# Two fused transformer blocks on one core: the keys' products regrouped by pairs of k-tiles under the modulation

## The chip, the cores and the metric

The kernel runs on one core of a Trainium2 chip, alone. The metric is device time in microseconds (us), the median of several executions; lower is better. Beside it stands one profiled execution, from which all rows below come.

## The reference

Two blocks follow each other. The first takes tokens `x` and a context `ctx`, each 256 x 1024, and two conditioning vectors, `c` and `c_ctx`. Cut to what the change touches:

```python
shift, scale, gate = split(silu(c) @ w_mod + b_mod)        # the same for c_ctx
h   = rmsnorm(x,   norm_w) * (1 + scale)   + shift
hc  = rmsnorm(ctx, norm_w) * (1 + scale_c) + shift_c
qkv, beta, decay, kb, vb = split(h @ w_state)              # the same for hc
q, k, v = silu(short_conv(qkv))                            # 4 heads of 128, conv of 5 taps
k = l2norm(k)
g, bt = gates(decay, beta)                                 # softplus, cumulative sums
o = gated_delta_rule(q, k, v, g, bt)                       # chunks of 64, both directions
...
x = x + gate * merge(...)
```

The second block (two feed-forward layers and a mixer, twice) takes `x` from there. It is not touched.

## The kernel before, in words

Everything is held transposed: 1024 features are 8 k-tiles (`KD`) of 128 partitions, and the 256 tokens (`T`) lie along the free axis. A product in fp32 accuracy is made of three fp32r matmuls: the weight is split into a high and a low part (`wload`: `wh` by an ACT copy, L98, `wl` by a DVE subtraction, L99) and so is the hidden tile (`split`, L289 and L290); `mm3` (L110 to L112) adds low x high, high x high and high x low. Weights arrive as panels of 512 KB (`wraw`, L90) through a ring of 7 buffers `raw`, issued by SP, and `wh` and `wl` have 4 buffers each. PSUM is 8 banks: `pj` 2, `ms` 2, `ch` 3, `md` 1.

The code is written in one order, and a scheduler then fixes one order of instructions for each engine. An engine works through its own list strictly in that order, so an instruction that waits holds up all that stand behind it on the same engine. `high_priority` (around the gates, the keys' convolution and the inverse) moves instructions ahead in those lists.

The first block opens with `b1_hidden`. `mod_row` (L729, L730) spreads silu(c) over all partitions. `mods(g)` makes shift and scale of two k-tiles, for g = 0 to 3: half of the shifts by multiply-and-reduce on DVE (L930), the rest by fp32 matmuls with the two conditioning columns `cc` as the stationary operand and a weight panel streaming (L943, result on 2 partitions), copied by ACT (L945) and transposed back (L948). `stats` squares the input (L155), sums the squares over features (`pss`, L165), takes the power on POOL (L170), spreads the result (`rb`, L173) and scales (L921). `hidden(g, ...)` applies scale and shift on ACT (L960) and splits.

Then come `b1_bd`, 48 products of 16 columns for the gates' inputs (L1022); `gates`, a chain of small DVE operations that ends in `gg` (L1111 to L1127), with sums over time on PE (`gps`, L1133; `gdf`, L1150) and exponentials `E` on ACT (L1151); and `b1_keys`, which for each of 4 heads takes 48 matmuls from `b1_both` (x and ctx, 8 k-tiles, 3 products), a convolution (`conv`: one ACT copy, L981, four DVE taps, L985, on both inputs at once), the halves of the key in chunk order (`conv_out`, L1001, or a silu on ACT for head 3, L999), 4 transposes (`ktp`, L1067), 4 squares with a sum (`ksq`, L1068) and 2 copies (L1069). `nke` (L1072) needs the sums of all four heads. From it follow `gc`, the products `Mc` (L1254), the triangular inverse of 32 x 32 blocks by 62 DVE operations `stmp` and `XW` (L1272, L1273), and the assembly of the full inverse on PE (`gx`, L1319; `gy`, L1325). Beside this chain PE works through two more such double products `w_kv` (each takes a `pj` bank), the four of `w_v`, and the 32 of `w_rest`.

```python
ps = self.b1_both(A["w_k"][h], hx, hc)      # b1_keys, per head
...
with self.tc.high_priority(offset=150):     # its convolution, transposes and squares
```

## Time and profile before

| what | value |
|---|---|
| median of 3 runs | 1453.55 us (1453.52 to 1453.86) |
| the profiled execution, its own time | 1454.4 us |
| span of its trace | 1452.6 us |
| PE busy | 1414.5 us, 97% of the span |
| DVE busy | 1149.1 us, 79% |
| ACT busy | 757.1 us, 52% |
| mean granted clock of PE | 0.995 |

The profile gives a page (busy time, 40 slices, the chain that ended last, the costliest groups) and answers to queries: the timeline of a stretch, the windows (busy time of each engine in given stretches), the waits of an engine by what ended them. Matmuls are pipelined: the duration of one is longer than its distance to the next, and PE counts as busy in both. The pace of PE is therefore read from starts, not from durations. An fp32 matmul leaves two records (two passes), an fp32r matmul one.

### The profile page before, as it was taken

To read this page: it belongs to the slowest core of one execution; us is meant where nothing else is said; L and a number is where in the kernel's file an instruction comes from. 1 tells how busy PE (TensorE), PEld (TensorE's weight loads), DVE (VectorE), ACT (ScalarE), POOL (GpSimd) and SP (SyncE) were. 2 spreads that over 40 slices of the span, in tenths; PEclk is the share of its full clock that TensorE was granted. 3 is DMA by queue.
4 is the path that set the end of the run, shared out by engine and by line. 5 is a ranking of instruction groups with operands and counts; after the bars stand their busy time and mean duration, and the time that the engine had idled before them with its cause. 6 is when DMAs were issued, how large, how long until landed. Compare 5 with 4: busy or idle time off the path is not lost. (4 is left out here: it accounts for less than half of the span.)

```text
span 1452.6 us, 27299 instructions
## 1 busy us (share of the span) xinstructions
PE 1414.5 (97%) x10738; PEld 1314.7 (91%) x10738; DVE 1149.1 (79%) x2130; ACT 757.1 (52%) x1285; POOL 90.4 (6%) x94
## 2 busy tenths in 40 slices
PE   7999889999999999999999999999999999999998
PEld 4799877789999988998899998999989998899997
DVE  6769777788887887898898788877778889896554
ACT  4653574354654455646664445554446347654442
POOL 0010100001300001001010001000001000100000
PEclk9999999999999999999999999999999999999999
DMA  8524544365688897456659898688775557577562
GB/s 325 183 60 124 152 131 120 99 197 187 213 261 278 298 320 226 160 160 215 205 151 318 279 337 263 185 282 290 244 242 180 174 168 240 173 241 245 177 197 70
DMA packets 94832, 303.96 MB, mean 209 GB/s; under 512 B 18128, under 2 KB 20432, under 8 KB 94448
## 3 DMA queue, kind: packets, MB, share of 16 engines
q1 hardware_dynamic: 89824, 299.90, 63.2%
q8 instruction: 84, 1.38, 0.4%
q10 hardware_dynamic: 4432, 1.11, 0.4%
q0 software_dynamic: 448, 1.21, 0.3%
q14 instruction: 44, 0.36, 0.1%
HBM read 300.09 MB, written 2.10 MB: 208 GB/s over the span
## 5 line engine op out<-in xcount | busy, mean ns | idle before, releaser
L98 ACT CAST wh<-raw 128x1024 fp32r<-128x1024 f32 (+3 forms) x407 | 414.6, 1021 | 280.7 <-PE psd L121 90.8
L99 DVE TENSOR_TENSOR wl<-raw,wh 128x1024 fp32r<-128x1024 f32 (+3 forms) x407 | 481.5, 1187 | 93.4 <-ACT wh L98 92.3
L111 PE MATMUL psf<-hH,wh 128*128 128x256 f32 x1088 | 306.1, 281 | 0.0
L112 PE MATMUL psf<-hL,wh 128*128 128x256 f32 x1088 | 305.6, 281 | 0.0
L110 PE MATMUL psf<-hH,wl 128*128 128x256 f32 x1088 | 305.5, 281 | 0.0
L121 PE MATMUL psd<-gHL,wh 128*128 128x512 f32 x704 | 244.3, 392 | 0.0
L739 DVE CUSTOM_DVE_ANT_0 raw<-raw,mrow 128x1024 f32<-128x1024 f32 x152 | 184.3, 1219 | 60.1 <-DMA raw<-in_wmod 59.8
L110 PEld LDWEIGHTS psf<-hH,wl 128*128 128x128 f32 x1088 | 205.6, 189 | 0.0
L112 PEld LDWEIGHTS psf<-hL,wh 128*128 128x128 f32 x1088 | 205.5, 189 | 0.0
L111 PEld LDWEIGHTS psf<-hH,wh 128*128 128x128 f32 x1088 | 204.8, 188 | 0.0
L122 PE MATMUL psd<-gHL,wl 128*128 128x256 f32 x704 | 196.8, 280 | 0.0
L121 PEld LDWEIGHTS psd<-gHL,wh 128*128 128x128 f32 x704 | 132.2, 188 | 29.1
L110 PE MATMUL psp<-hH,wl 128*128 128x256 f32 x512 | 148.9, 291 | 2.8 <-DVE wl L99 2.3
L111 PE MATMUL psp<-hH,wh 128*128 128x256 f32 x512 | 147.8, 289 | 0.0
L112 PE MATMUL psp<-hL,wh 128*128 128x256 f32 x512 | 147.4, 288 | 0.0
L122 PEld LDWEIGHTS psd<-gHL,wl 128*128 128x128 f32 x704 | 132.1, 188 | 0.0
L110 PEld LDWEIGHTS psp<-hH,wl 128*128 128x128 f32 x512 | 97.4, 190 | 5.0 <-PE psp L112 1.6
L112 PEld LDWEIGHTS psp<-hL,wh 128*128 128x128 f32 x512 | 97.3, 190 | 1.1 <-issue 0.7
L111 PEld LDWEIGHTS psp<-hH,wh 128*128 128x128 f32 x512 | 97.0, 189 | 0.4 <-issue 0.2
L249 ACT ACTIVATE ft<-psf 128x256 f32<-128x256 f32 x68 | 26.1, 383 | 110.0 <-PE psf L112 110.0
L157 POOL TENSOR_TENSOR sqa<-sqa,sq 128x256 f32<-128x256 f32 x36 | 31.2, 866 | 591.9 <-issue 480.6
L110 PE MATMUL psk<-hH,wl 128*128 128x256 f32 x160 | 46.7, 292 | 2.3 <-DVE cvv L985 2.3
(517 smaller groups left out, 2805.0 us busy)
## 6 DMA issues: line engine op xcount, KB each, us to landing
raw<-in_ffn_gu SPq DMA_DIRECT2D x176, 512.0 KB, 4.4
raw<-in_wmod SPq DMA_DIRECT2D x144, 512.0 KB, 4.5
raw<-in_ffn_dn SPq DMA_DIRECT2D x64, 448.0 KB, 4.2
raw<-in_win SPq DMA_DIRECT2D x56, 512.0 KB, 4.4
raw<-in_w_rest SPq DMA_DIRECT2D x32, 512.0 KB, 3.7
raw<-in_ffn_dn SPq DMA_DIRECT2D x32, 512.0 KB, 4.5
raw<-in_wmod_sc SPq DMA_DIRECT2D x12, 512.0 KB, 8.3
raw<-in_wout_a SPq DMA_DIRECT2D x16, 384.0 KB, 3.8
```

What stands on the lines that cost most here:

```text
L98: nc.scalar.copy(H[:, :n], raw[:, :n])
L99: nc.vector.tensor_sub(L[:, :n], raw[:, :n], H[:, :n].bitcast(F32))
L110: mm(ps, L[:, s], hH[:, b, :T], start=f, stop=False)
L111: mm(ps, H[:, s], hH[:, b, :T], start=False, stop=False)
L112: mm(ps, H[:, s], hL[:, b, :T], start=False, stop=l)
L121: mm(ps, H[:, s], h[:, b, :, :T], start=first and i == 0, stop=False)
L122: mm(ps[:, 1, :], L[:, s], h[:, b, 0, :T], start=False, stop=last and i == len(kw) - 1)
L157: self.seng.tensor_add(self.sqa, self.sqa, o)
L249: nc.scalar.activation(t, ps[:, 0, :], AF.Silu)
L739: nc.vector.tensor_tensor_reduce(raw, raw, row, op0=ALU.mult, op1=ALU.add, scale=1.0, scalar=0.0, accum_out=t[:, j : j + 1])
```

## The change

In `b1_hidden` all shifts and scales now come from matmuls. `mods(g)` holds the conditioning columns 32 wide (`c2`, 30 of the 32 columns zero), and for each of 2 kinds and 2 panels issues 4 matmuls whose results go to 4 different groups of 32 PSUM partitions. The copy to SBUF (L936) takes all 128 partitions, and a product with a selector `sel` (L941) adds the four groups and turns the result back. The second spread row (`crow`) and the DVE reductions are gone. x is loaded ahead of the first panels.

The keys' weights are laid out by pairs of k-tiles (`w_kg`), and `products(g)` multiplies two k-tiles for all 4 heads and for the gates (60 fp32r matmuls) into 5 open PSUM banks `acc`: both `pj`, the `md` and two `ch`. It is called for g - 1 after `mods(g)`, and for 3 at the end. `b1_bd` and `b1_keys` read `acc` in place of making the products. In the new file these functions stand 4 to 10 lines lower (the taps are L995, the halves L1011, `gg` L1131, `gps` L1137, `gdf` L1154, `E` L1155, `ktp` L1071, `ksq` L1072, `nke` L1076).

```diff
@@ -902,15 +902,17 @@
         xs = self.nrm.tile([P, KD, T], F32, tag="xs", name="xs")
         self.c1 = self.silu_cols("c", 8)
         cc = self.silu_cols("c_ctx", 8)
-        c2 = pb.tile([P, KD, 2], F32, tag="gg", name="cc2")
+
+        c2 = pb.tile([P, KD, 32], F32, tag="E0", name="cc2")
+        nc.vector.memset(c2, 0.0)
         nc.vector.tensor_copy(c2[:, :, 0], self.c1)
         nc.vector.tensor_copy(c2[:, :, 1], cc)
+        sel = pb.tile([P, 2], F32, tag="gy", name="sel2")
+        nc.vector.reduce_sum(sel, self.ident.rearrange("p (g c) -> p c g", g=4)[:, 0:2, :], axis=AX.X)
+        mm = pb.tile([P, 2, KD, 2], F32, tag="gp", name="mm1")
+        mA = pb.tile([P, KD, 2], F32, tag="gg", name="mA1")
+        out = [self.parts(0), self.parts(1)]
         self.rows = [self.mod_row(self.c1)]
-        rows = self.rows[0], self.mod_row(cc, pb.tile([P, 1024], F32, tag="E1", name="crow"))
-        junk = pb.tile([P, 1024], F32, tag="E0", name="mjk")
-        mm = pb.tile([P, 2, KD, 2], F32, tag="gp", name="mm1")
-        mA = pb.tile([P, KD, 2], F32, tag="gy", name="mA1")
-        out = [self.parts(0), self.parts(1)]
 
         def stats(x, o):
             self.stat_open(x, None, None, None)
@@ -920,57 +922,65 @@
             for k in range(0, KD, 2):
                 nc.vector.tensor_mul(o[:, k : k + 2, :], x[:, k : k + 2, :], rb[:, None, :T].broadcast_to([P, 2, T]))
 
-        def mods(g, after=None):
-            a = slice(2 * g, 2 * g + 2)
-            fast = g % 2 == 0
-            if fast:
-                for k in (2 * g, 2 * g + 1):
-                    raw = self.wraw(self.A["wmod_sh"][g + k % 2], 1024)
-                    for i in range(2):
-                        nc.vector.tensor_tensor_reduce(raw if i else junk, raw, rows[i], op0=ALU.mult, op1=ALU.add, scale=1.0, scalar=0.0,
-                                                       accum_out=mm[:, 0, k, i : i + 1])
+        def mods(g):
+
+
+            ps = self.chbank("psm1").rearrange("p (k t) -> p k t", t=T)
+            for kind in range(2):
+                for i in range(2):
+                    raw = self.wraw(self.A["wmod_s"][4 * g + 2 * kind + i], 1024)
+                    for j in range(4):
+                        nc.tensor.matmul(ps[32 * j : 32 * j + 32, kind, :], c2[:, 4 * i + j, :], raw[:, j * T : (j + 1) * T],
+                                         start=i == 0, stop=i == 1, skip_group_check=True)
+            row = pb.tile([P, 2, T], F32, tag="tg", name="mrow", bufs=2)
+            nc.scalar.copy(row, ps)
             t = self.msbank("m1t")
-            for kind in range(int(fast), 2):
-                ps = self.pj.tile([P, 2, T], F32, tag="pj", name="psm1")
-                o = ps[0:2, 0, :]
-                raws = [self.wraw(self.A["wmod_sc"][2 * (2 + g if kind else g // 2) + i], 1024) for i in range(2)]
-                if after:
-                    nc.sync.dma_start(after[0], self.A[after[1]])
-                    after = None
-                for i, raw in enumerate(raws):
-                    for j in range(4):
-                        k = 4 * i + j
-                        nc.tensor.matmul(o, c2[:, k, :], raw[:, j * T : (j + 1) * T], start=k == 0, stop=k == 7)
-                row = pb.tile([P, T], F32, tag="tg", name="mrow", bufs=2)
-                nc.scalar.copy(row[0:2, :], o)
+            for kind in range(2):
                 for j in range(2):
                     n = 4 * kind + 2 * j
-                    nc.tensor.transpose(t[:, n : n + 2], row[0:2, j * P : (j + 1) * P], self.ident[0:2, 0:2])
-            for kind in range(2):
-                d = mm[:, kind, a, :]
-                src = d if fast and not kind else t[:, 4 * kind : 4 * kind + 4].rearrange("p (a b) -> p a b", b=2)
-                nc.vector.tensor_add(d, src, self.v("b_mod", 8 * kind + 2 * g, 2)[:, :, None].broadcast_to([P, 2, 2]))
+                    nc.tensor.matmul(t[:, n : n + 2], row[:, kind, j * P : (j + 1) * P], sel, start=True, stop=True)
+            a = slice(2 * g, 2 * g + 2)
+            nc.vector.tensor_add(mm[:, :, a, :], t[:, 0:8].rearrange("p (k a b) -> p k a b", k=2, b=2),
+                                 self.v("b_mod", 0, 16).rearrange("p (k c) -> p k c", k=2)[:, :, a, None].broadcast_to([P, 2, 2, 2]))
             nc.vector.scalar_tensor_tensor(mA[:, a, :], mm[:, 1, a, :], 1.0, self.v("norm_w", 2 * g, 2)[:, :, None].broadcast_to([P, 2, 2]),
                                            op0=ALU.add, op1=ALU.mult)
 
-        def hidden(g, sets):
-            for i in sets:
+        def hidden(g):
+            for i in range(2):
                 xr, (H, L) = (xs, ctxT)[i], out[i]
                 for k in (2 * g, 2 * g + 1):
                     nc.scalar.activation(xr[:, k, :], xr[:, k, :], AF.Identity, scale=mA[:, k, i : i + 1], bias=mm[:, 0, k, i : i + 1])
                     self.split(H[:, k, :T], L[:, k, :T], xr[:, k, :])
 
-        mods(0, (self.xT, "x"))
-        mods(1, (ctxT, "ctx"))
+        def products(g):
+
+            W = self.wload(self.A["w_kg"][g])
+            for h in range(5):
+                for s in range(2):
+                    for j in range(2):
+                        k = 2 * g + j
+                        (WH, WL), w = (W, slice((2 * h + j) * P, (2 * h + j + 1) * P)) if h < 4 else (W_bd, slice(16 * k, 16 * k + 16))
+                        o = acc[h][:, s, :] if h < 4 else acc[h][0:16, s, :]
+                        hH, hL = (a[:, k, :T] for a in out[s])
+                        for i, (x, y) in enumerate(((WL, hH), (WH, hH), (WH, hL))):
+                            nc.tensor.matmul(o, x[:, w], y, start=k + s + i == 0, stop=k == 7 and i == 2, skip_group_check=True)
+
+        nc.sync.dma_start(self.xT, self.A["x"])
+        mods(0)
+        nc.sync.dma_start(ctxT, self.A["ctx"])
         stats(self.xT, xs)
+        W_bd = self.wload(self.A["w_bd"], P)
+        acc = [p.tile([P, 2, T], F32, tag=t, name="psk")
+               for p, t in ((self.pj, "pj"), (self.pj, "pj"), (self.md, "md"), (self.ch, "ch"), (self.ch, "ch"))]
         stats(ctxT, ctxT)
-        mods(2)
-        hidden(0, (0,))
-        mods(3)
         self.seng = nc.gpsimd
-        hidden(0, (1,))
-        for g in (1, 2, 3):
-            hidden(g, (0, 1))
+        hidden(0)
+        for g in range(1, 4):
+            mods(g)
+            products(g - 1)
+            hidden(g)
+        products(3)
+        self.acc = acc
         return out
 
 
@@ -1013,13 +1023,7 @@
         self.cwh = pb.tile([P, 60], F32, name="cwh")
         nc.vector.tensor_scalar(self.cwh, self.v("conv_w"), 0.5, None, op0=ALU.mult)
         gb = pb.tile([P, 2, 4, 8], F32, name="gb")
-        H, L = self.wload(self.A["w_bd"], P)
-        ps = self.pj.tile([P, 2, T], F32, tag="pj", name="psb")
-        for s, h in enumerate((hx, hc)):
-            for k in range(KD):
-                w = slice(16 * k, 16 * k + 16)
-                for i, (a, b) in enumerate(((L, h[0]), (H, h[0]), (H, h[1]))):
-                    nc.tensor.matmul(ps[0:16, s, :], a[:, w], b[:, k, :T], start=k + i == 0, stop=k == 7 and i == 2)
+        ps = self.acc[4]
         y = pb.tile([P, 2, T], F32, tag="ksq", name="gby", bufs=2)
         nc.scalar.copy(y[0:16], ps[0:16])
         tp = self.msbank("gbt")
@@ -1052,7 +1056,7 @@
         self.kt = [pb.tile([P, 2, 4, P], F32, tag="kt" + n, name="kt" + n) for n in "xc"]
         self.vp = [pb.tile([P, 2, 4, P], F32, tag="vp" + n, name="vp" + n) for n in "xc"]
         for h in range(4):
-            ps = self.b1_both(A["w_k"][h], hx, hc)
+            ps = self.acc[h]
             if h % 2 == 0:
                 cv = pb.tile([P, 2, 2, 2, T], F32, tag="conv", name="cvk")
             with self.tc.high_priority(offset=150):
...
-    A["wmod_sh"] = np.concatenate([panelR(w[:, g * T : (g + 1) * T]) for g in (0, 2)])
-    A["wmod_sc"] = np.concatenate([panelV(w[:, g * T : (g + 1) * T]) for g in (1, 3, 4, 5, 6, 7)])
+    A["wmod_s"] = np.concatenate([panelV(w[:, (4 * kind + g) * T : (4 * kind + g + 1) * T]) for g in range(4) for kind in range(2)])
...
-    A["w_k"], A["w_v"] = panelT(k), panelT(v)
+    A["w_kg"] = np.ascontiguousarray(panelT(k).reshape(4, P, 4, T).transpose(2, 1, 0, 3).reshape(4, P, 1024))
+    A["w_v"] = panelT(v)
```

What it moves shows at three places of the engines' lists. First the opening on PE, up to the first sums of squares (`pss`); `psm1` are modulation products, `m1t` the turned results. Before:

```order
L943 MATMUL psm1_160<-raw_161,cc2_115 2x256 x4
L943 MATMUL psm1_160<-raw_163,cc2_115 2x256 x4
L729 MATMUL mr_416<-ident_86,sc_c_2_411 128x128 x2
L943 MATMUL psm1_182<-raw_183,cc2_115 2x256
L948 MATMUL m1t_159<-ident_86,mrow_174 128x2 x2
L943 MATMUL psm1_182<-raw_183,cc2_115 2x256 x3
L943 MATMUL psm1_182<-raw_185,cc2_115 2x256 x4
L729 MATMUL mr_416<-ident_86,sc_c_2_411 128x128 x2
L729 MATMUL mr_422<-ident_86,sc_c_2_411 128x128
L948 MATMUL m1t_181<-ident_86,mrow_196 128x2 x2
L165 MATMUL pss_242<-ones_88,sqa_220 128x1 x2
```

Now:

```order
L933 MATMUL psm1_141<-raw_142,cc2_115 32x256 x4
L933 MATMUL psm1_141<-raw_148,cc2_115 32x256 x4
L933 MATMUL psm1_141<-raw_154,cc2_115 32x256 x4
L933 MATMUL psm1_141<-raw_160,cc2_115 32x256 x4
L941 MATMUL m1t_168<-sel2_119,mrow_166 128x2 x4
L165 MATMUL pss_198<-ones_88,sqa_176 128x1 x2
L165 MATMUL pss_198<-ones_88,sq_196 128x1 x2
L173 MATMUL rb_207<-ident_86,nr_205 128x128 x2
L933 MATMUL psm1_275<-raw_276,cc2_115 32x256 x4
L933 MATMUL psm1_275<-raw_282,cc2_115 32x256 x4
L165 MATMUL pss_247<-ones_88,sqa_225 128x1 x2
L165 MATMUL pss_247<-ones_88,sq_245 128x1 x2
```

Ahead of the first `pss` there are now all 16 products of the first group, with their copy and turn, and the context's `pss` stands between the two halves of the second group.

Second the gates on DVE, from `gy` to the chain that ends in `gg`; `cvk` are the keys' taps, `kTx` and `kTc` the halves of a key, `wl` the low part of a weight panel. Before:

```order
L1113 TENSOR_TENSOR gy_445<-gb_457,vec_84 128x32
L1115 SCALAR_TENSOR_TENSOR gu_446<-gy_445 128x32
L1112 TENSOR_SCALAR gbe_444<-gbe_444 128x32
L1125 TENSOR_SCALAR gy_445<-gy_445 128x32
L1117 TENSOR_SCALAR gd_447<-gu_446 128x32
L1118 RECIPROCAL gd_447<-gd_447 128x32
L1119 TENSOR_TENSOR gu_446<-gu_446,gd_447 128x32
L1120 TENSOR_TENSOR gd_447<-gu_446 128x32
L1121 TENSOR_SCALAR gp_448<-gd_447 128x32
L1123 SCALAR_TENSOR_TENSOR gp_448<-gp_448,gd_447 128x32 x5
L985 SCALAR_TENSOR_TENSOR cvk_646<-psk_591,cwh_455,cvk_646 128x2x254
L1123 SCALAR_TENSOR_TENSOR gp_448<-gp_448,gd_447 128x32
```

Now:

```order
L1011 SCALAR_TENSOR_TENSOR kTx_796<-cvk_847 128x2x64 x2
L1011 SCALAR_TENSOR_TENSOR kTc_797<-cvk_847 128x2x64 x2
L1036 COPY gb_723<-gbt_726 64x16
L1037 COPY gb_723<-gbt_726 64x2x8
L1038 COPY gb_723<-gbt_726 64x2x8
L99 TENSOR_TENSOR wl_1274<-raw_1271,wh_1273 128x1024
L1116 TENSOR_SCALAR gbe_710<-gbe_710 128x32
L1117 TENSOR_TENSOR gy_711<-gb_723,vec_84 128x32
L1119 SCALAR_TENSOR_TENSOR gu_712<-gy_711 128x32
L1129 TENSOR_SCALAR gy_711<-gy_711 128x32
L99 TENSOR_TENSOR wl_1355<-raw_1352,wh_1354 128x1024
L1121 TENSOR_SCALAR gd_713<-gu_712 128x32
```

Before, the gates' chain stood ahead of the first taps. Now all taps of four heads, three heads' halves and four splits of weights stand ahead of it.

Third the exponentials `E` and the keys' squares on ACT; `gdf` and `ktp` are PE's results that they read. Before:

```order
L1151 ACTIVATE E_560<-gdf 128x512 x2
L1151 ACTIVATE E_559<-gdf 128x512 x2
L1068 ACTIVATE ksq,nke<-ktp 128x128 x2
L1069 COPY ktx<-ktp 128x2x128
L1068 ACTIVATE ksq,nke<-ktp 128x128 x2
L1069 COPY ktc<-ktp 128x2x128
L990 ACTIVATE cvk<-cvk 128x512
L1068 ACTIVATE ksq,nke<-ktp 128x128 x2
L1069 COPY ktx<-ktp 128x2x128
L1068 ACTIVATE ksq,nke<-ktp 128x128
L981 ACTIVATE cvk<-psk,cwh 128x512
```

Now:

```order
L1120 ACT_TABLE_LOAD
L1120 ACTIVATE gu<-gu 128x32
L1141 ACTIVATE eg<-gps 128x128
L1155 ACTIVATE E_771<-gdf 128x512 x2
L1155 ACTIVATE E_770<-gdf 128x512 x2
L1072 ACTIVATE ksq,nke<-ktp 128x128 x3
L1073 COPY ktx<-ktp 128x2x128
L1072 ACTIVATE ksq,nke<-ktp 128x128
L1073 COPY ktx<-ktp 128x2x128
L1072 ACTIVATE ksq,nke<-ktp 128x128 x3
```

Before, the squares of a head stood between the copies and splits of later heads' products. Now all 16 squares stand behind the four exponentials, and no head's products are left beside them.

## Rows read from the trace of the kernel before

**Rows 1.** The page: engines, busy us (share), instructions; one group: busy, mean ns.

```profile
PE 1414.5 (97%) x10738; PEld 1314.7 (91%) x10738; DVE 1149.1 (79%) x2130; ACT 757.1 (52%) x1285; POOL 90.4 (6%) x94
...
L98 ACT CAST wh<-raw 128x1024 fp32r<-128x1024 f32 (+3 forms) x407 | 414.6, 1021 | 280.7 <-PE psd L121 90.8
```

**Rows 2.** Windows: PE, PEld, DVE, ACT, POOL busy us; granted clock, DMA share, GB/s.

```profile
10.00:20.00 10.00, 10.00 (x56) 4.89 (x54) 6.49 (x17) 5.09 (x13) 0.00 (x0) 1.00 1.01 415
...
30.00:40.00 10.00, 8.59 (x38) 4.00 (x39) 7.03 (x18) 4.03 (x11) 1.28 (x2) 0.83 0.81 232
...
130.00:140.00 10.00, 9.53 (x80) 9.32 (x79) 10.00 (x21) 4.99 (x11) 1.82 (x1) 1.00 0.31 103
```

**Rows 3.** Timeline of the opening: start us, us, engine, line, what, count [idle].

```profile
12.90 0.42 ACT L155 ACTIVATE sqa<-xT 128x256 f32<-128x256 f32 x1 [1.71 <-DMA xT<-in_x]
...
16.48 0.95 ACT L155 ACTIVATE sq<-xT 128x256 f32<-128x256 f32 x2 [0.74 <-DVE sqa L157]
...
19.61 0.61 PE L165 MATMUL pss<-ones,sqa 128*128 128x1 f32 x4
...
22.45 2.48 DVE L921 TENSOR_TENSOR xs<-xT,rb 128x512 f32<-128x512 f32 x4 [1.59 <-PE rb L173]
22.56 3.62 PE L943 MATMUL psm<-raw,cc 128*2 128x256 f32 x16
...
31.39 0.52 PEld L165 LDWEIGHTS pss<-ones,sqa 128*128 128x128 f32 x4 [2.00 <-issue]
...
37.35 0.69 ACT L289 CAST hH<-ctxT 128x256 fp32r<-128x256 f32 x2
```

**Rows 4.** Timeline of PE: two products to different halves of the PSUM partitions.

```profile
651.91 0.65 PE L356 MATMUL pv<-sw,vz 128*64 128x256 f32 x4
652.39 0.38 PE L357 MATMUL pv<-sw,vz 128*64 128x128 f32 x2
```

**Rows 5.** Timeline of PE: first and last of the 48 gate products.

```profile
45.27 0.29 PE L1022 MATMUL psb<-hH,wl 128*16 128x256 f32 x1 [0.93 <-DVE wl L99]
...
50.80 0.28 PE L1022 MATMUL psb<-hL,wh 128*16 128x256 f32 x1
```

**Rows 6.** Timeline of DVE, PE and ACT: the gates, 55 to 69 us.

```profile
55.83 0.18 DVE L1117 TENSOR_SCALAR gd<-gu 128x32 f32<-128x32 f32 x1
...
57.10 1.09 DVE L1123 SCALAR_TENSOR_TENSOR gp<-gp,gd 128x32 f32<-128x32 f32 x5
...
62.09 0.58 PE L1133 MATMUL gps<-gg,Ctri 128*128 128x16 f32 x4
...
68.47 0.60 ACT L1151 ACTIVATE E<-gdf 128x512 f32<-128x512 f32 x1 [0.26 <-PE gdf L1150]
```

**Rows 7.** Timeline of DVE: halves of a key, keys' taps, a split of weights.

```profile
72.77 0.49 DVE L1001 SCALAR_TENSOR_TENSOR kTx<-cvk 128x128 f32<-128x128 f32 x2 [1.57 <-ACT cvk L990]
...
76.60 1.53 DVE L985 SCALAR_TENSOR_TENSOR cvk<-psk,cwh,cvk 128x508 f32<-128x508 f32 x2 [2.93 <-ACT cvk L981]
78.07 1.22 DVE L99 TENSOR_TENSOR wl<-raw,wh 128x1024 fp32r<-128x1024 f32 x1
```

**Rows 8.** Timeline of ACT and DVE: the keys' squares, and what follows from them.

```profile
70.79 0.28 ACT L1068 ACTIVATE ksq<-ktp 128x128 f32<-128x128 f32 x1 [0.42 <-PE ktp L1067]
...
71.58 0.28 ACT L1068 ACTIVATE ksq<-ktp 128x128 f32<-128x128 f32 x1 [0.42 <-PE ktp L1067]
...
91.67 0.30 ACT L1068 ACTIVATE ksq<-ktp 128x128 f32<-128x128 f32 x1
91.94 0.39 ACT L1069 COPY ktx<-ktp 128x256 f32<-128x256 f32 x1
...
94.57 0.17 DVE L1072 TENSOR_SCALAR nke<-nke 128x16 f32<-128x16 f32 x1 [1.16 <-ACT ksq L1068]
...
162.84 0.19 DVE L1273 TENSOR_TENSOR XW<-XW,stmp 128x31 f32<-128x31 f32 x1
```

**Rows 9.** Waits of PE, 150 to 200 us: us in total, times, longest.

```profile
PE gx L1319 <- issue: 5.2, 2, 4.5
```

## The prediction

> **What bounds the kernel now.** I read the page first, then the windows of the first 200 us, then timelines of single stretches, then the waits. The page gives PE 97% of the span [rows 1], which points to PE everywhere; but a busy share counts overlapping matmuls in full, and it does not tell what PE waits for when it waits. The windows [rows 2] show DVE full for the whole of 130 to 140 us. There it runs the triangular inverse between splits of weights. That inverse cannot begin before `nke`, the squared lengths of all four heads' keys, at 94.57 us, and its last step ends at 163.0 us [rows 8]. Behind it PE, which has by then used up the projections that it can do without the inverse, waits 5.2 us in the assembly of the inverse [rows 9]. So from about 55 to 175 us there are two chains side by side: PE's projections, and the chain gates, keys, `nke`, inverse. The second ends last. The first block is therefore worth what the change does to the time of `nke`, not what it does to PE's work.
>
> **The opening, up to the first key product.** Before, the first fp32r product starts at 45.27 us [rows 5]. Now x is loaded ahead of the first four panels, but x and these panels are the same 3.4 MB that lay up to x before, so the fourth panel lands when x landed, at 12.9 us [rows 3]; at 415 GB/s [rows 2] no order makes that shorter. PE's list puts the 16 products of this group, their copy and their turn (about 0.5, 0.6 and 0.9) ahead of x's `pss`: 15.0 us, in place of 19.61. From `pss` to the first scaling were 2.84 us [rows 3], so 17.9. ACT's list has one modulating activation of x ahead of the context's squares; they begin at 19.2. x's eight squares took from 12.90 to 17.43 [rows 3]; with four more ACT steps among them I take 5.2, so the context's `pss` comes at 24.4 in place of 31.39. From there to the second `hH` of the context were 6.65 us (31.39 to 38.04) [rows 3]: 31.1. ACT and DVE then copy the second group's row (0.6) and split the first key panel (1.0 and 1.2) [rows 1, 7]. The first key product starts at 33.9, **11.4 us earlier** than before.
>
> **The modulation products.** One pass of 256 columns takes 0.226 us (16 in 3.62) [rows 3]. Before, 96 passes made 21.7 us; now there are 64 matmuls, 128 passes, 28.9 us in a line. But results go to four groups of partitions. The only row of this kind is a pair that writes the two halves: four passes in 0.48 us, where a line would take 0.90 [rows 4]. Two run abreast in full; four at once no row shows. Bounds for one group of 16: 7.2 us in a line, 3.6 in pairs, 1.8 four abreast. The pair lost nothing, so I take 1.8. The Trainium skill (TensorE: Matmul & The Clock Gate, Part 3) gives 2.38 times for three column tiles, a little under their number; by it a group would take some 2.3 us and the sum would grow by 1 us.
>
> **Key products.** 48 products take 5.53 us between first and last, 0.118 each [rows 5], so `products(g)` with 60 takes 7.1. Before it PE has been used thinly. In 30 to 40 us the mean granted clock was 0.83 [rows 2]: a third of it at 1.2 instead of 2.4 GHz, which loses 1.7 us; I charge this once. Each later group's modulation lies on PE between two products, with 0.9 for its turn: the start of `products(3)` is 33.9 + 7.1 + 1.7 + 1.8 + 8.0 + 1.8 + 8.0 = **62.3 us**, its end 69.4. The copies, splits and modulating activations between (some 6 us of ACT and DVE a group) are hidden by the 7 us of the product before; without that cover each would cost up to 1 us. The panels of the last group can only be issued when `raw` buffers come free, at the second group's products (42.7 us), and land 4 to 5 us later, under `products(1)`.
>
> **What is no longer covered.** Before, the gates' chain and the taps of one head ran under the products of the next. Now k is the outer loop: no head is ready before 62.3 + 1.4 us, and then all four come within 6 us. DVE's list puts ahead of the end of the gates (`gg`), from 62.3 us on: 2.4 us until the first taps can begin (one split, and ACT's copy), 16 taps at 0.735 (two in 1.47) = 11.8; four splits at 1.14 = 4.6; three heads' halves, 12 at 0.22 = 2.7 [rows 7]; 8 small copies and 4 small steps, 1.7; the wait for ACT's exponential, 0.4; the chain from `gd` to `gg`, 2.4 up to its fifth polynomial step and 1.3 for the last four [rows 6]. Together 27.3, so `gg` at 89.6 us. Meanwhile PE has the rest of `products(3)` (7.1), the spread row and small turns (2.5) and two double products (11.4): 21.0 us. **PE then stands idle about 6 us**. The four products of `w_v` are ready as data, but stand behind `gps` in PE's list.
>
> **Behind the gates.** From `gps` to the end of the last exponential `E` were 7.0 us (62.09 to 69.07) [rows 6]: 96.6. All 16 squares and 8 copies on ACT stand behind it. A square alone takes 0.27, a copy up to 0.39 [rows 8]: 7 us if ACT is never kept waiting; at the pace at which they ran before, each waiting for its transpose (0.79 apart) [rows 8], 12.6. Heads now alternate between banks, so I take 8, near the lower bound. `nke` comes at **104.6 us, 10.0 later** than before.
>
> **The sum.** From `nke` on the lists are nearly the same and DVE is full, so the delay carries through to 175 us and PE waits for it. One split of `w_v` has moved ahead of `nke`, which gives 1.2 back [rows 7]. PE's own work falls by some 15 us (21.7 to 7.2; 16 half-length passes of the second spread row, 1.8; against 1 more for the turns), but it is PE that waits. Later nothing changes. So +8.8 us: the profiled execution's own 1454.4 becomes 1463.2; its median was 0.85 below it, so **1462.4 us**. What measurement can tell from no change is about 0.2%, 2.9 us. Unknown costs in the sum: the opening -3 to +4, the modulation 0 to +3.6 (pairs), the squares -1 to +4.6, the taps and splits -3 to +2, together about -6 to +8.
>
> **A rule on the clock.** The trace shows full clock up to 30 us, with PE in use, and the fall only after a thin stretch [rows 2]. The Trainium skill (TensorE: Matmul & The Clock Gate, Part 1) holds that the lower level is the default and that activity lifts it. The opening now has 3.6 us of modulation passes where it had 21.7; by the rule it would run at the lower level as a whole, its small products on the path (about 5.8 us: spreads, turns, sums) would double, and the result would be near 1468. No row here has an opening so thin.
>
> **Rivals.**
> *The chain meshes and PE is the bound after all (faster).* The point that decides is the way from `products(3)` to `nke`: under 32.3 us instead of 42.3 and nothing is lost, under 29 and the gain can be measured. For that the low ends of all bounds (-6) must hold, and the four splits and some 4 us of the taps must fall into waits that I counted beside them (-9): `nke` at 89.6, 5.0 earlier, and with the 1.2 of the split -6.2, **1447.3**. For it speaks that PE has 15 us less to do and is 97% busy [rows 1]. Against it: the items are 27 us of DVE work in one strict list. 0.16.
> *The delay is soaked up.* If PE's wait in the assembly [rows 9] hangs on PE's own order as well, only the 3 us or less of PE's own lateness reach the end: **1455**. 0.10.
> *The four groups do not run abreast (it doesn't do what it says).* Then two groups of 7.2 instead of 1.8 lie between the products, and the opening is 1.5 us later: +12, **1475**. The pair in the trace speaks against it [rows 4]. 0.06.
> *Forecast.* Cover lost, `nke` later: 1456 to 1470. 0.68.
>
> **How the numbers follow.** Slower by over 0.2% are forecast and the third rival, 0.74; within 0.2% the second, 0.10; faster the first, 0.16. The range reaches from 1450, which leaves out most of the faster case, to 1471, which leaves out the serial one: about 0.2 together.
>
> **What the new profile would show.** First key product near 34 us; each group's 32 modulation passes in about 1.8 us, four starting together; `products(3)` from about 62 us; PE idle some 6 us ahead of `gps` near 84 to 90 us; `nke` near 105 us; PE's wait in the assembly not shorter than before. I am wrong if `nke` comes before 97 us, or if it comes late and the assembly on PE does not.

## The result, and the profile after

The changed kernel takes **1469.89 us** (median of 4 runs, 1468.32 to 1476.59); the kernel before, on the same chip, 1453.7. The ratio is 1.0113, with a 95% interval of 1.009 to 1.0136: slower by some 16 us. The prediction said 1462.4, within 1450 to 1471, and slower with 0.74. The profiled execution took 1470.08 us, its span 1468.3.

The page of the changed kernel answers to [rows 1]: PE is no less busy, in a longer span.

```profile
PE 1415.5 (96%) x10774; PEld 1322.2 (90%) x10774; DVE 1141.2 (78%) x2112; ACT 766.0 (52%) x1289; POOL 88.7 (6%) x94
```

The opening of the changed kernel, timeline of PE (start us, us, line, what, count, idle before it):

```profile
11.19 0.64 PE L933 MATMUL psm<-raw,cc 128*32 128x256 f32 x8 [0.64 <-DMA raw<-in_wmod_s]
...
13.45 0.58 PE L165 MATMUL pss<-ones,sqa 128*128 128x1 f32 x4
...
32.59 0.58 PE L966 MATMUL psk<-hH,wl 128*128 128x256 f32 x1 [1.60 <-DVE wl L99]
...
42.43 1.93 PE L933 MATMUL psm<-raw,cc 128*32 128x256 f32 x32
```

The 32 modulation passes of a group take 1.93 us: four column groups do run abreast. x's `pss` comes at 13.45 instead of 19.61 [rows 3] and the first key product at 32.59 instead of 45.27 [rows 5], 12.7 us earlier. Behind it, timelines of PE, DVE and ACT:

```profile
90.02 1.01 PE L1137 MATMUL gps<-gg,Ctri 128*128 128x16 f32 x4 [6.02 <-issue]
...
89.73 0.19 DVE L1131 SCALAR_TENSOR_TENSOR gg<-gy,gea 128x32 f32<-128x32 f32 x1
...
107.69 0.17 DVE L1076 TENSOR_SCALAR nke<-nke 128x16 f32<-128x16 f32 x1 [10.62 <-ACT ksq L1072]
...
98.35 0.60 ACT L1155 ACTIVATE E<-gdf 128x512 f32<-128x512 f32 x1 [0.48 <-PE gdf L1154]
```

`gg` comes 28 us later than before (89.73 against 61.82), PE has stood idle 6.02 us ahead of `gps`, and `nke` is at 107.69 instead of 94.57 [rows 8]. The windows of the changed kernel (columns as in [rows 2]), and of the kernel before at the same time:

```profile
10.00:20.00 10.00, 6.23 (x52) 3.62 (x52) 3.64 (x11) 3.09 (x9) 0.70 (x1) 0.72 1.03 411
...
30.00:40.00 10.00, 8.40 (x49) 8.32 (x50) 4.37 (x9) 5.08 (x10) 0.00 (x0) 0.66 0.61 206
...
80.00:90.00 10.00, 4.01 (x34) 3.81 (x34) 7.95 (x31) 5.50 (x10) 0.15 (x1) 0.80 0.32 105
90.00:100.00 10.00, 9.35 (x25) 5.28 (x25) 2.81 (x5) 3.56 (x12) 0.00 (x0) 0.69 0.09 27
100.00:110.00 10.00, 8.15 (x32) 6.05 (x33) 2.19 (x9) 7.53 (x37) 2.05 (x1) 0.66 0.01 2
```

```profile
90.00:100.00 10.00, 9.72 (x82) 9.26 (x81) 6.49 (x17) 4.05 (x13) 5.41 (x2) 1.00 0.18 54
```

From 80 to 110 us PE has 91 records of matmuls; before, it had 82 in the ten us from 90 alone. The granted clock is 0.66 to 0.80 there (1.2 GHz for a good part); it was full. Where the delay went from there is read at the first update of the residual, `xT<-pso`, in the output projection that closes the first block. The kernel before, then the changed one:

```profile
366.72 0.48 DVE L213 SCALAR_TENSOR_TENSOR xT<-pso,gate,xT 128x256 f32<-128x256 f32 x1 [0.49 <-PE pso L112]
```

```profile
379.59 0.48 DVE L213 SCALAR_TENSOR_TENSOR xT<-pso,gate,xT 128x256 f32<-128x256 f32 x1 [0.49 <-PE pso L112]
...
740.00:750.00 10.00, 8.49 (x58) 7.87 (x59) 7.22 (x13) 5.13 (x10) 4.17 (x5) 0.91 0.29 105
...
1280.00:1290.00 10.00, 9.78 (x69) 9.58 (x68) 7.31 (x16) 7.56 (x11) 0.46 (x1) 0.83 0.36 112
```

So 12.9 us of the 15.7 by which the spans differ are lost in the first block. Matched instructions of ACT show the rest: two steps of 1.5 us, near 740 and 1275 us, where the granted clock dips in this execution. The waits of PE in the assembly of the inverse (total, times, longest) answer to [rows 9]:

```profile
PE gx L1323 <- issue: 4.8, 1, 4.8
```

PE waits as long as before, so the delay of `nke` reached the end of the block almost whole.

### The profile page after: what moved, and what is told of

Its sections match the earlier page's. It is cut to its first block, busy times and chain, and to the rows that moved or that the text cites. A ratio compares the mean times of both kernels' runs of the same rounds, so it can differ in the third digit from the quotient of the medians.

```text
span 1468.3 us, 27366 instructions
## 1 busy us (share of the span) xinstructions
PE 1415.5 (96%) x10774; PEld 1322.2 (90%) x10774; DVE 1141.2 (78%) x2112; ACT 766.0 (52%) x1289; POOL 88.7 (6%) x94
## 5 line engine op out<-in xcount | busy, mean ns | idle before, releaser
L194 PE MATMUL psu<-xL,wh 128*128 128x258 f32 x160 | 46.2, 289 | 1.8 <-DVE xL L153 1.8
```

Source lines behind the costliest of these rows:

```text
L194: mm(ps[:, : T + 2], a[:, w], b[:, k, :], start=k + i == 0, stop=k == KD - 1 and i == 2)
```

## Experiments

The theories. **Lost cover** (mine): gates, taps and squares come behind all key products, with nothing beside them. **Slow clock**: a thin PE falls to 1.2 GHz, and that is the loss. **The new modulation** itself, or its loads, is the loss. The table gives, of each kernel's profiled execution, the start in us of `gg`, `nke`, the inverse's first `stmp` and the first `xT<-pso`; then the median in us, and the ratio to the kernel before, run beside it (1453.6 to 1454.6 us), with its interval.

| kernel | gg | nke | stmp | xT<-pso | median | ratio |
|---|---|---|---|---|---|---|
| before | 61.82 | 94.57 | 114.95 | 366.72 | 1453.7 | 1 |
| changed | 89.73 | 107.69 | 128.41 | 379.59 | 1469.89 | 1.0113 (1.009 to 1.0136) |
| changed, again | 90.08 | 107.69 | 128.53 | 380.85 | 1468.76 | 1.0108 (1.0091 to 1.0125) |
| 1 modulation alone, by head | 61.42 | 96.75 | 118.63 | 371.81 | 1463.65 | 1.0058 (1.0044 to 1.0073) |
| 2 both, gates first | 75.12 | 94.62 | 115.21 | 367.94 | 1457.82 | 1.0032 (1.0019 to 1.0044) |
| 3 gates' columns first only | 88.59 | 106.13 | 126.58 | 379.00 | 1467.9 | 1.0096 (1.0077 to 1.0115) |
| 4 gates' lists first only | 83.22 | 103.80 | 130.85 | 381.92 | 1471.97 | 1.0109 (1.0092 to 1.0126) |
| 5 fill ahead of gps | 90.38 | 105.43 | 129.10 | 379.01 | 1468.39 | 1.0094 (1.0076 to 1.0111) |
| 6 fill in the opening | 87.73 | 105.39 | 131.38 | 383.03 | 1471.71 | 1.0121 (1.0106 to 1.0137) |
| 7 modulation in a line | 100.85 | 118.60 | 145.40 | 396.64 | 1486.85 | 1.0223 (1.0208 to 1.0238) |
| 8 mixed | 75.29 | 93.62 | 114.76 | 365.54 | 1454.74 | 1.0002 (0.9991 to 1.0013) |
| 9 mixed, modulation ahead | 73.89 | 92.56 | 113.81 | 366.69 | 1457.47 | 1.002 (1.0011 to 1.0029) |
| 10 the same with fill | 70.47 | 89.16 | 110.17 | 362.86 | **1450.07** | 0.9969 (0.9959 to 0.9979) |
| 11 by head, with fill | 63.20 | 98.53 | 118.98 | 372.92 | 1462.08 | 1.0049 (1.0037 to 1.0062) |

**The changed kernel again**, without an edit.

> The changed kernel once more, unaltered, beside the others of this batch. In its first profile nke stood 13.1 us behind that of the kernel before, the first feed-forward layer started 12.7 us later, and 3.0 us more were lost near 740 and 1275 us, where the granted clock fell and did not in the profile of before. If the first loss is the change's and the second the run's: nke at 107.7 and the layer's delay at 12.7 again within 0.5, while the later 3.0 may come out as anything from 0 to 4; median 1468 to 1471. If both are the change's: all of it repeats within 0.5.

Measured: `nke` at 107.69 again, the first block 14.1 us late (12.9), and nothing lost behind it:

```profile
740.00:750.00 10.00, 8.15 (x63) 7.32 (x62) 7.52 (x13) 5.73 (x13) 5.38 (x6) 1.00 0.41 119
1280.00:1290.00 10.00, 9.79 (x82) 9.58 (x81) 8.62 (x18) 8.29 (x12) 0.48 (x1) 1.00 0.50 152
```

What is lost up to `nke` is the change's. The two late steps belong to the execution. In the first block the two differ by 1.3 us, more than the 0.5 expected, so of the four numbers in the table `xT<-pso` is the least sharp.

**1. The modulation alone.**

```diff
-            products(g - 1)
...
-        products(3)
...
-            ps = self.acc[h]
+            ps = self.b1_both(A["w_k"][h], hx, hc)
```

The gates' 48 products `psb` come back as they were, too.

> One part of the change alone: the new modulation (four column groups, x loaded first), while the gates' columns and the four heads are multiplied as before, all k-tiles of one after the other, the gates first. Lost cover (mine): what cost time is that gates, taps and squares come behind all key products, so with the old order of products the opening's gain should be left over. The panels need some 36 us to land (18 transfers, 10.5 MB at the 300 GB/s of the first slice), so the gates' first product falls near 42 instead of 45.27, nke near 91.5 instead of 94.57, and the time is 1450.5 us (1447 to 1453.5). The new modulation or the new order of loads is itself the cost: at or over 1460. The thin, slow PE of the opening is the cost: 1453 to 1457, since PE is as thin here until 42.

A miss: 1463.65 instead of 1450.5, and over the 1460 from which on the new modulation or its loads were to be blamed. Kernels 2 and 8 speak against that: they have the same modulation and loads, and take 1457.82 and 1454.74. The gates' first product starts at 45.48, no earlier than before [rows 5], and goes at the low clock:

```profile
45.48 0.40 PE L1013 MATMUL psb<-hH,wl 128*16 128x256 f32 x1 [4.46 <-DVE wl L99]
...
49.94 0.42 PE L1013 MATMUL psb<-hH,wl 128*16 128x256 f32 x1
```

By head, all k-tiles must be ready before anything starts; the four rounds of panel, row copy, turn, activation and split take until 45 us. So the 12.7 us earlier first key product come from the regrouping, which needs only the first group, and hardly from the products side by side: kernel 7, regrouped but with the products in a line, starts its first key product at 34.01, 1.4 us behind the changed kernel. The 21 intervals from 45.48 to 49.94 are 0.21 us each instead of 0.118; all 48 products last 7.8 us instead of 5.65, which is as much as `nke` is late (2.2 us). Another 2.9 us are lost from `nke` to `xT<-pso`, 1.7 of them on a way through DRAM (last section). The median is some 4 us worse than that; why, no run here settles.

**2 to 4. The order of the gates.** The same work, grouping and loads; only PE's column order, the lists' priority, or both.

```diff
-            for h in range(5):
+            for h in (4, 0, 1, 2, 3):                       # 2 and 3
-            gb = self.b1_bd(hx, hc)
-            for _ in self.prior(gates(gb), 600):
+            with self.tc.high_priority(offset=900):         # 2 and 4
+                gb = self.b1_bd(hx, hc)
+            for _ in self.prior(gates(gb), 900):
```

> The change with nothing but the order of its lists altered: in each group the gates' columns are multiplied ahead of the heads', and the gates' chain has offset 900 instead of 600, so that DVE takes it in turns with the taps of the first two heads rather than behind all four. PE's work, the loads and the grouping by k-tiles stay. Lost cover: gg falls near 79 instead of 89.73, E is done near 89 and the squares of the first heads run while DVE has the taps of the last two; nke near 99 instead of 107.7, time 1461 us (1457 to 1465). If it is the regrouping of the products (when the heads are whole) and not the order behind it: within 2 us of the change, 1468 to 1472. If the slow clock behind gps is what matters: half of it, 1465 to 1468, with gps to the last E still at about 9 us.

> The change with nothing but the gates' columns multiplied ahead of the heads' in each group; the lists keep offset 600. It is the fourth corner beside the change, the lists alone (1472) and both (1457.8). The two only help together (the gates' inputs must be there early and DVE must take them first): DVE's list keeps all four heads' taps ahead of the gates' chain, so gg stays within 2 us of 89.7, nke within 2 us of 107.7, time 1466.5 to 1471. The columns alone do it: gg near 80, nke near 99, time 1458 to 1462.

> The change with the gates' chain moved ahead in the lists alone (offset 900 instead of 600, also for the transposes ahead of it); the gates' columns are still multiplied behind the heads' in each group. It splits the gain of the kernel that had both. Both parts count: the chain begins near 72 as in the change, runs in turns with the taps instead of behind them, gg near 82.5 instead of 89.7 (and 75.1 with both), nke near 101, time 1463.5 us (1461 to 1466). The order of PE's products was all of it: gg stays near 89, 1468 to 1470. The lists were all of it: nke near 95, 1456.5 to 1459.

Both together bring `nke` back to 94.62 and the time to 1457.82: 12 of the 16 us, by order alone, and more than expected (99 and 1461). Of the other 4 us, 1.2 are lost by `xT<-pso`; the rest lies behind the first block and is not explained. Kernel 2, timeline of DVE and windows:

```profile
75.12 0.19 DVE L1132 SCALAR_TENSOR_TENSOR gg<-gy,gea 128x32 f32<-128x32 f32 x1
94.62 0.18 DVE L1077 TENSOR_SCALAR nke<-nke 128x16 f32<-128x16 f32 x1 [0.90 <-ACT ksq L1073]
...
80.00:90.00 10.00, 10.00 (x70) 8.33 (x68) 7.35 (x14) 8.27 (x30) 0.00 (x0) 1.00 0.23 66
90.00:100.00 10.00, 8.52 (x68) 7.47 (x66) 6.40 (x15) 7.53 (x30) 2.90 (x1) 1.00 0.19 55
```

The clock is full where it was 0.80 and 0.69, with no matmul added: the slow clock is what the lost cover does to PE. Neither half does it alone. The columns give 1.6 us at `nke` (DVE still takes all taps first). The lists give 3.9 us there, and nothing at the end: that expectation (1463.5) was a miss, for the reasons that kernel 6 shows (here `cvv` waited 4.0 us for PE, and the way through DRAM took 6.4).

**5 and 6. Fill.** fp32 matmuls whose results nobody reads: ten in the 6 us ahead of `gps` (5; by `be`, `u` and `d` as operands), or eight in the opening (6, the diff).

```diff
+                nc.tensor.matmul(acc[0][0:32, 0, :], c2[:, 0, :], a[:, k, :], start=True, stop=True)
...
+        warm(xs, (2, 3, 4, 5, 6))
         stats(ctxT, ctxT)
...
+            if g == 1:
+                warm(ctxT, (4, 5, 6))
             products(g - 1)
```

> The change with ten fp32 matmuls (32 x 256) added, whose results nobody reads, put by what they read (gbe, gu, gd) into the 6 us that PE waits ahead of gps; they take about 4.5 us at full clock. Nothing else moves. Slow clock as a cost of its own: with PE busy from 83.5 to 88 the granted clock of 80 to 100 us rises from 0.80 and 0.69 to near 1.0, gps to the last E goes from 8.9 back to 7.0 us, nke from 107.7 to near 105.5, time 1467.5 us. Lost cover alone, clock of no account there: nke stays at 107.7 within 0.5, time 1469.5 to 1470.5. If the added matmuls run at the low clock, they end behind gg: gps starts up to 3 us later, time 1471 to 1473.

> The change with eight fp32 matmuls (32 x 256) added whose results nobody reads (into the bank of head 0 before its first product), five ahead of the context's sum of squares and three ahead of the first key products; every order stays. Slow clock in the opening as a part of the loss: the first group's products take 7.1 to 7.5 us instead of 9.8, all behind it moves up by 2 to 3 us, nke to 105 to 105.7, time 1466 us (1465 to 1467.5). Lost cover alone, PE waiting for panels or splits anyway: nke within 0.7 of 107.7, time 1468 to 1470.

Both brought `nke` 2.3 us forward, as the slow clock predicts; neither brought the end forward by more than the two executions of the changed kernel differ. (In kernel 6 the first group's products took 8.8 us, from 31.59 to 40.43; 7.1 to 7.5 were expected, and the changed kernel again took 8.8 as well, from 33.94 to 42.78. The gain lies in the earlier start.) Windows of kernel 5:

```profile
80.00:90.00 10.00, 8.77 (x59) 6.46 (x58) 7.90 (x28) 5.54 (x11) 0.15 (x1) 1.00 0.30 103
90.00:100.00 10.00, 8.42 (x33) 4.10 (x31) 3.36 (x8) 5.78 (x25) 0.00 (x0) 0.96 0.10 31
100.00:110.00 10.00, 9.21 (x41) 7.78 (x40) 4.39 (x13) 5.30 (x25) 2.90 (x1) 0.53 0.00 0
```

The low stretch moved: 0.53 from 100 to 110 us, where the changed kernel had 0.66 and its repeat 1.00 (with 0.56 in the ten us before). What a low stretch costs there is read on ACT and SP, in kernel 6 and below it in the changed kernel with DVE's part of `Dg` (`Dg` is the second half of the blocks to be inverted, made by ACT and DVE; `dr` is its way through DRAM, `XW` its return):

```profile
119.15 0.69 ACT L998 ACTIVATE cvv<-psk,vec 128x512 f32<-128x512 f32 x1 [3.97 <-PE psk L112]
...
120.67 1.65 ACT L1273 COPY Dg<-Mc 32x256 f32<-32x256 f32 x4
122.35 0.37 ACTq L1275 DMA_DIRECT2D dr<-Dg  x1
...
127.70 0.45 SPq L1276 DMA_DIRECT2D XW<-dr  x1
```

```profile
118.59 0.69 ACT L991 ACTIVATE cvv<-psk,vec 128x512 f32<-128x512 f32 x1 [2.60 <-PE psk L112]
...
119.11 1.79 DVE L1267 STREAM_TRANSPOSE Dg<-Mc 32x256 f32<-32x256 f32 x4
...
120.12 1.64 ACT L1266 COPY Dg<-Mc 32x256 f32<-32x256 f32 x4
121.79 0.37 ACTq L1268 DMA_DIRECT2D dr<-Dg  x1
...
125.06 0.45 SPq L1269 DMA_DIRECT2D XW<-dr  x1
```

In ACT's list the first value head's `cvv` stands ahead of this `Dg`, and waits for the first product of `w_v`, which PE makes behind `gps`, at the low clock where the stretch is low. So a second chain (`gps`, PE, `w_v`, `cvv`, ACT's part of `Dg`) runs about as late as the one by `nke` and DVE's part: in the changed kernel it ends 0.9 us behind it (121.76 and 120.90), in the repeat 0.3 us ahead of it. Shortening the one by `nke` alone gives nothing. On top, the way through DRAM took 5.4 us instead of 3.3 (last section).

**7. Modulation in a line.**

```diff
-                        nc.tensor.matmul(ps[32 * j : 32 * j + 32, kind, :], c2[:, 4 * i + j, :], raw[:, j * T : (j + 1) * T],
-                                         start=i == 0, stop=i == 1, skip_group_check=True)
+                        nc.tensor.matmul(ps[0:32, kind, :], c2[:, 4 * i + j, :], raw[:, j * T : (j + 1) * T],
+                                         start=i + j == 0, stop=i + j == 4, skip_group_check=True)
```

> The change with the modulation's matmuls all sent to the same 32 PSUM partitions, so that the eight of a kind accumulate one behind the other; copy and selector take 32 partitions. It prices the four column groups. Passes in a line cost 0.226 us each (as in the kernel before), 7.2 us a group instead of the 1.93 measured, 5.3 us more. Groups 2 and 3 stand between the products in PE's order, groups 0 and 1 partly hide under the panels' arrival: lost cover and PE's order give gg and nke some 11 us later than in the change (118) and 1481 us (1475 to 1487). If the panels' arrival hides it: nke within 3 us of the change's, 1469 to 1473. If a PE that is kept busy in the opening runs at the full clock there and gains it back: 1472 to 1477, with a granted clock near 1.0 from 30 to 40 us.

```profile
34.01 0.39 PE L966 MATMUL psk<-hH,wl 128*128 128x256 f32 x1
...
42.83 7.09 PE L933 MATMUL psm<-raw,cc 128*32 128x256 f32 x32
```

7.09 us against 1.93, 5.2 more for each of the two groups that stand between products; `nke` 10.9 us later, as expected. The end is 17 us later, six more than that. They are lost from `nke` to `stmp` (26.8 us instead of 20.7), at the two places that kernel 6 shows: `cvv` waited 4.0 us for PE, and the way through DRAM took 6.1.

**8 to 10. Towards a better kernel.** Kernel 8 keeps two groups under the modulation, and multiplies k-tiles 4 to 7 column block by column block, gates first, with the gates' lists first.

```diff
+            if g < 3:
                 products(g - 1)
...
-        products(3)
+        Ws = [self.wload(self.A["w_kg"][g]) for g in (2, 3)]
+        for h in (4, 0, 1, 2, 3):
+            for g in (2, 3):
+                part(g, (h,), Ws[g - 2])
```

> The change with its first two groups of k-tiles under the modulation as it has them, but k-tiles 4 to 7 multiplied column block by column block (gates, then head 0, 1, 2, 3), and the gates' chain moved ahead in the lists (offset 900 instead of 600, also for the transposes ahead of it). Lost cover: the gates' columns are whole some 11 us earlier than in the change (58.5 instead of 69.7), gg some 13 us earlier (76), the heads follow 2.8 us apart, nke falls near 96 and the time is 1455.5 us (1451 to 1460). The clock behind the gates is the cost, whatever the order: nke moves by the same as the products do and no more, 1465 or over.

As expected: `nke` 93.62, and the time of the kernel before. Kernel 9 puts `mods(2)` ahead of the first products and `mods(3)` ahead of the second; kernel 10 adds the fill of kernel 6, written to the gates' bank instead of head 0's (and the gates' columns of its first two groups come ahead of the heads'). The diff is against kernel 8 with its loop written out.

```diff
         mods(1)
+        mods(2)
         products(0)
         hidden(1)
-        mods(2)
+        mods(3)
         products(1)
         hidden(2)
-        mods(3)
         hidden(3)
```

> The mixed kernel (two groups of k-tiles under the modulation, then gates and heads column block by column block, the gates' chain ahead in the lists) with the modulation's third group multiplied ahead of the first products and its fourth ahead of the second products, as soon as panels allow, instead of behind them. Lost cover: k-tiles 4 to 7 are then ready near 48 us instead of 60, the gates' columns are whole near 54 instead of 61.7, gg at 68 instead of 75.3, and the rest of the heads' products covers the gates' chain; nke near 90 instead of 93.6, time 1451 us (1447 to 1454). If the squares set the end (PE's total is unchanged, so head 3 comes out no earlier and its taps, silu and squares follow): nke 92.5 to 94, 1453.5 to 1456.

> The kernel of the previous line with eight fp32 matmuls (32 x 256) added whose results nobody reads, five ahead of the context's sum of squares and three ahead of the first key products, where PE waits. Slow clock as a cost of its own: the granted clock of 30 to 40 us (0.60 to 0.66 with products by groups) rises to 0.9 or more, the first 24 or so key products take 0.118 us instead of 0.21, and nke comes 2 us earlier than without them, time 2 us lower. Clock of no account for the end (what PE gains it waits for at the next panels): nke and time within 0.7 us of the kernel without them.

Kernel 9: `gg` only 1.4 us earlier, not 7, `nke` where the second theory has it, and 1457.47, above both. The third group in a slow opening put its first key product at 38.21 instead of 34.10. Windows and PE's timeline of kernel 9, then of kernel 10:

```profile
20.00:30.00 10.00, 6.54 (x37) 3.89 (x37) 5.57 (x14) 4.38 (x12) 0.70 (x1) 0.66 0.61 210
30.00:40.00 10.00, 5.58 (x48) 4.66 (x49) 4.27 (x12) 7.66 (x18) 0.00 (x0) 0.80 0.81 311
...
38.21 0.58 PE L970 MATMUL psk<-hH,wl 128*128 128x256 f32 x1 [1.60 <-DVE wl L99]
...
46.05 0.28 PE L970 MATMUL psk<-hH,wl 128*16 128x256 f32 x1
```

```profile
20.00:30.00 10.00, 8.53 (x67) 4.75 (x67) 5.86 (x14) 4.50 (x12) 0.70 (x1) 0.90 0.83 268
30.00:40.00 10.00, 8.54 (x79) 5.71 (x79) 4.11 (x12) 7.85 (x18) 0.00 (x0) 0.95 0.76 252
...
31.37 0.29 PE L970 MATMUL psk<-hH,wl 128*16 128x256 f32 x1
...
36.40 0.28 PE L970 MATMUL psk<-hL,wh 128*16 128x256 f32 x1
...
38.14 0.38 PE L970 MATMUL psk<-hH,wl 128*128 128x256 f32 x1 [1.46 <-DVE wl L99]
...
89.16 0.17 DVE L1093 TENSOR_SCALAR nke<-nke 128x16 f32<-128x16 f32 x1 [1.80 <-ACT ksq L1089]
```

With the fill `nke` is 3.4 us earlier, `xT<-pso` 3.8, and the median 7.4 us lower than without. The clock is the smaller part of the 3.4. Half of the gates' 48 products (16 columns wide, `128*16`) ran from 31.37 to 36.40, while PE waited for what the first product of a head needs; in kernel 9 all 48 come behind the heads' first products, from 46.05 on. By estimate that takes 24 x 0.118 = 2.8 us out of the way, while the first product of a head is no earlier (38.14 and 38.21) and the 48 of the first group take 7.2 us instead of 7.7. This order came with the fill; what either would give alone was not tried. The profiled execution of kernel 10 was its slowest (1453.66 us), so no trace shows what the median gains beyond the first block. **Kernel 10 is faster than both kernels of this case**, 1450.07 us.

**11. Fill by head.** Kernel 1 with fourteen such matmuls.

```diff
+        warm(xs, (2, 3, 4, 5, 6))
         stats(ctxT, ctxT)
...
+            if g == 1:
+                warm(ctxT, (4, 5, 6))
             hidden(g)
+        warm(self.xT, range(6))
```

> The kernel with the new modulation alone (products by head, gates first), with fourteen fp32 matmuls (32 x 256) added whose results nobody reads, where PE waits in the opening. In the kernel without them the gates' first 23 products took 0.21 us each instead of 0.118, which is the whole 2.2 us by which its nke is late. Slow clock is what the modulation alone costs: the gates' 48 products take 5.7 us, nke falls near 94.6 as in the kernel before, time 1456 to 1459.5. The longer chain of panel, copy, selector and splits is what costs: nke stays near 96.7, 1462 to 1465.

Inconclusive. The fill stood in the way of the last modulation group, so the first product came at 47.89, and the clock of 40 to 50 us was 0.72 all the same. Whether a full clock would give kernel 1 back its loss is open.

## Why the prediction was right or wrong

The sign, the mechanism and its place were right; the size was 7.5 us short, with the result inside the range. In the profiled execution some 3 us of that are missing at `nke`, 1.2 in a term that was to be given back, and 3 in the two late steps.

- *Opening.* Right to 1.6 us: 13.45, 22.87 and 32.59 us for 15.0, 24.4 and 33.9.
- *Modulation group, four abreast at 1.8 us.* Right: 1.93. The Trainium skill (TensorE: Matmul & The Clock Gate, Part 3) gives 2.38 times for three column tiles; four here gave 7.09 / 1.93 = 3.7, so the estimate of 2.3 us a group that was worked out from it was too long.
- *`products(3)` and `gg`.* Right to 0.5 us: the last product ends at 69.89 (69.4), `gg` at 89.92 (89.6), and PE is idle for 6.02 us (about 6).
- *"From `gps` to the end of the last exponential `E` were 7.0 us".* **Mis-sized**: 90.02 to 98.95, 8.9 us (in the repeat 9.8). I took the duration from a stretch at full clock, and put it behind 6 us of idle PE; the clock there was 0.69. In kernel 5, with PE kept busy, it is 5.9 us.
- *Squares, "I take 8".* 8.7 us (in the repeat 7.5). With the two, `nke` is 13.1 us late and not 10.0.
- *"One split of `w_v` has moved ahead of `nke`, which gives 1.2 back."* **Failed**: the inverse starts 13.5 us late (13.6 in the repeat). From `nke` to the end of DVE's second `Dg` pass 13.2 us in the kernel before (94.57 to 107.79) as in the changed one (107.69 to 120.90), and no split stands among these steps in either, so there was nothing to give back. The wait of ACT's `cvv` on PE cost up to 0.9 us in the first execution and nothing in the repeat.
- *"Later nothing changes."* The two late steps of the profiled execution, 3 us together, did not come again; the repeat supports the sentence.
- *"PE's own work falls by some 15 us".* The page doesn't show it (busy 1414.5 before, 1415.5 now); busy time also grows with the low clock.
- *The bounds.* Those listed add up to -7 and +14; "about -6 to +8" doesn't follow from them by a sum.
- *"I charge this once"* (the clock, 1.7 us in the opening). That was the root of the mis-sized `E`: the clock was low behind `gg` too. *The rule on the clock* (Trainium skill, TensorE: Matmul & The Clock Gate, Part 1: the lower level is the default, and activity lifts it) agrees with the opening: granted 0.72, 0.60 and 0.66 from 10 to 40 us, where before it was full up to 30. The 1468 estimated by it lies near the result for another reason: the first key product was not late, and the loss lies behind `gg`.

The second `Dg` on DVE in the kernel before and in the repeat of the changed one (in its first execution, see kernel 6):

```profile
106.00 1.79 DVE L1263 STREAM_TRANSPOSE Dg<-Mc 32x256 f32<-32x256 f32 x4
```

```profile
119.12 1.79 DVE L1267 STREAM_TRANSPOSE Dg<-Mc 32x256 f32<-32x256 f32 x4
...
120.99 0.37 ACTq L1268 DMA_DIRECT2D dr<-Dg  x1
```

The rivals: "meshes" is refuted (`nke` 107.69, not 89.6), "soaked up" too (the first block is 12.9 us late, not 3), and "not abreast" by kernel 7, which shows its price. Lost cover is shown by kernel 2: the same work in another order takes 12 us off.

## What to carry to other kernels

Making k the outer loop starts the products early but makes all results whole at the same time: what consumes them then runs uncovered, so the consumer with the longest chain must come out first and be first in every list, both at once. A duration taken from a busy stretch doesn't hold behind an idle one: charge the low clock in every stretch that the change makes thin. And when one chain is shortened without effect, look at the list of the engine where the next thing waits, for a step of another chain ahead of it.

## What the runs showed of the hardware

- Eight small matmuls without use raised the granted clock of 20 to 30 us from 0.60 (0.67 in the repeat) to 0.91 in kernel 6 and from 0.66 to 0.90 in kernel 10. In kernels 5 and 6 the fill brought `nke` 2.3 us forward and the end not at all. Kernel 10 is 7.4 us faster than kernel 9, but the fill came with another order of the gates' products, which by estimate accounts for 2.8 of the 3.4 us at `nke`.
- The way of 256 KB through DRAM (`dr<-Dg` to the issue of `XW`) took 3.0 us for the first half in all 14 profiled executions. For the second half SP issues a 512 KB panel nearby: in kernels 4 to 7, from 0.3 us ahead of it to 0.3 us behind, it took 5.2 to 6.4 us; in the other ten, 1.0 to 1.9 us behind, 3.2 to 3.7 in eight, but 4.4 in kernel 9 and 4.9 in kernel 1. So the panel's time goes with it and is not all of it; that the panel is the cause was not tried.
- The granted clock dips near 740 and 1275 us in one execution of a kernel and not in the next, 1.5 us each.
